# The end of the attention, w_ob and w_out under a hand-written order, with w_out as Strassen's seven products

## The chip, the cores and the metric

The kernel runs on one core of a Trainium2 chip. The metric is device time in microseconds (us) of one execution. The other quantities below come from one execution that the hardware profiler recorded; its span runs from the first to the last instruction, and its own time is a little longer than that span.

The core has TensorE (PE, the matrix engine; its loads of the stationary operand are shown as PEld), VectorE (DVE), ScalarE (ACT), GpSimd (POOL) and SyncE (SP). Here SP only issues transfers. All of them run at once and wait for each other through semaphores. SBUF is the on-chip memory, PSUM holds the matrix engine's results.

## The reference, cut to what matters

One layer has two branches over 1024 latent tokens of width 1024, and 256 context tokens that are only read. Branch A is a gated DeltaNet, branch B a differential softmax attention with 8 heads. Both end in the same way:

```python
y_a = rms_norm(o_a, gdn_norm_w) * silu(z_a)                     # (1024 tokens, 1024)
y_b = rms_norm(o_b, diff_norm_w) * (1 - lambda_init) * silu(z_b)
merged = g_a * (y_a @ w_oa) + g_b * (y_b @ w_ob)                # g_a, g_b: sigmoid gates
out = x + gate * (merged @ w_out)                               # gate: one number per channel
```

w_oa, w_ob and w_out are 1024 x 1024, and everything is float32. This case is about the last two lines and the last head of the attention.

## The kernel before, in words

**Matrix products.** A float32 operand is split in two: hi is a copy rounded to the type that PE reads fast (fp32r), lo is the rest. ACT makes hi, and DVE or POOL makes lo by a subtraction. A product then takes three matmuls for each 128 input channels: hi·hi, hi·lo and lo·hi. All matmuls go through `mm` (L55), all transposes through `tr` (L58); the profile therefore shows them under these two lines, and they are told apart by the names of their tiles.

**Order.** The work of the attention is written as generators ("streams"). Each one yields an instruction with its engine, an estimate of its time and what it waits for. `turn_flow` keeps a clock for each engine and always emits the instruction that can start earliest; the bias of a stream decides between those that could start at the same moment. So the order on each engine is fixed when the kernel is built, and on the chip each engine runs its own list in order. The estimates distinguish `DVE` from `DV2` (a DVE instruction with two SBUF operands, which is not planned beside one of POOL), and `DMA` is issued by SP.

**The attention.** For each of 8 heads and each of 8 blocks of 128 queries, `scores` (tile s) makes both score matrices over 1280 keys, `score_out` (L1557) evacuates them, `soft` (L1570) takes the exponential, `scale` (L1587) and `add` (L1594) combine the two maps, `turns` transposes the result (tile t, L58), `high` and `low` split it (L1626, L1631), and `att_out` multiplies it with the values (tile v). When a head has all its blocks, `norm_` computes the inverse norm (POOL, tile bry, L172), turns it (tile m, L58), sends it through memory to spread it over the partitions (rbd, rr), multiplies the head (POOL, L1714) and stores it in `yb`.

**w_oa.** `merge_` multiplies branch A's heads with w_oa beside the attention, in 16 groups (2 halves of 512 tokens times 8 blocks of 128 output channels) of 24 matmuls with 512 moving columns (tile ma), using one PSUM bank, `pbank`. `merge_out` gates a group and stores it in memory (`ma`). With `KEEP = 3` the last three groups are left over.

**The end, `phase3`.** It starts when the hand-written order is over and has its own pools. Here the tile framework orders the work. It runs the three left groups of w_oa (`branch_a`, L1814); it loads every head from `yb` (L1865) and splits it (L1868 on ACT, L1869 alternately on POOL and DVE); then w_ob follows in 16 groups of 24 matmuls (tile m, 512 columns), each with a gate and an addition on DVE (L1896, L1897) and a split of the merged result (L1898, L1899). w_out then comes in four stretches of 256 output channels (tile mo): for each block of 128 tokens 24 matmuls with 256 moving columns, whose sum DVE multiplies with the gate (L1920) and POOL or DVE adds to x (L1925, L1922), before it is stored. The splits of w_ob and w_out are in `split_small` (L1823, L1824).

Of the kernel before, what the change touches and what calls it, by code (L numbers as in the profile page):

```python
# [17 lines left out]
P = 128  # L18
# [7 lines left out]
H = 8  # L26
# [17 lines left out]
class Block:  # L44
# [665 lines left out]
    def run(self):  # L710
# [4 lines left out]
        with ExitStack() as left:  # L715
# [981 lines left out]
    def norm_(self, h, w, t, to):  # L1697
# [4 lines left out]
        yield lambda: self.pbank  # L1702
        b = self.pbank.pop(0)
        pm = self.pm.tile([P, 512], F32, tag="mm", name="m")
# [3 lines left out]
        self.pbank.append(e)  # L1708
# [3 lines left out]
        for k in range(4):  # L1712
            s = slice(k * W, (k + 1) * W)
            t = yield POOL, 0.69, [e, to], lambda: nc.gpsimd.tensor_tensor(w["oT"][:, s], w["oT"][:, s], rr[:, s], ALU.mult)  # L1714
        self.rrfree = t
        self.kept[h] = yield DMA, 1.46, [t], lambda: nc.sync.dma_start(self.yb[h], w["oT"])
# [33 lines left out]
    def side_weights(self):  # L1750
# [11 lines left out]
        for i, p in enumerate(todo):  # L1762
# [39 lines left out]
    def branch_a(self, o, m):  # L1802

        nc = self.nc
        os = slice(o * 512, o * 512 + 512)
        g = self.yr.tile([P, 512], F32, tag="g", name="g")
        nc.sync.dma_start(g, self.gt[m][:, os])
        _, hi, lo = self.ready_["a", o, m]
        pt = self.pm.tile([P, 512], F32, tag="mm", name="ma")
        for k in range(KT):  # L1810
            _, yh, yl = self.ready_["y", o, k]
            for i, (x, y) in enumerate(((hi, yh), (hi, yl), (lo, yh))):
                self.mm(pt, x[:, k], y, k == i == 0, k == KT - 1 and i == 2)
        nc.vector.tensor_tensor(g, pt, g, ALU.mult)  # L1814
        nc.sync.dma_start(self.ma[m][:, os], g)

    def split_small(self, raw, shape):

        nc, n = self.nc, shape[0] // 2
        hi, lo = (self.ws.tile([P, *shape], F32R, tag=t, name=t) for t in ("wh", "wl"))  # L1820
        for s in range(2):
            k = slice(s * n, s * n + n)
            nc.scalar.copy(hi[:, k], raw[:, k])  # L1823
            (nc.vector, nc.gpsimd)[s].tensor_tensor(lo[:, k], raw[:, k], hi[:, k].bitcast(F32), ALU.subtract)  # L1824
        return hi, lo

    def load_small(self, src):
        raw = self.wr.tile([P, KT, P], F32, tag="wr", name="wr")
        self.nc.sync.dma_start(raw, src.rearrange("(k p) n -> p k n", p=P))
        return self.split_small(raw, (KT, P))  # L1830

    def phase3(self, side):

        nc, a = self.nc, self.a
        with ExitStack() as st:
            mp, yr = self.spool(st, "mp", side="right"), self.spool(st, "yr3", 2, side="right")
            self.wr = self.spool(st, "wr3", 2, side="right")
            self.pm = self.spool(st, "pm3", 6, space=PSUM)
            mh, ml = {}, {}
            left = [(g, a["w_oa"][0, :, g[2] * P:(g[2] + 1) * P]) for g in self.groups]  # L1840
            left += [(("b", m), a["w_ob"][0, :, m * P:(m + 1) * P]) for m in range(KT)]
            for o in range(2):
                for h in range(H):
                    assert ("y", o, h) in self.ready_
            wt = {}

            def fetch(i):
                if i < len(left):
                    g, src = left[i]
                    wt[g] = self.ready_[g][1:] if g in self.ready_ else self.load_small(src)  # L1850

            def out_load(u):
                ws = self.ws
                self.ws = wf if u % 2 == 0 else ws
                raw = wf.tile([P, KT, W], F32, tag="wr", name="wr", bufs=1)
                nc.sync.dma_start(raw, a["w_out"][0, :, u * W:(u + 1) * W].rearrange("(k p) n -> p k n", p=P))
                wt["o", u] = [self.split_small(raw[:, k:k + 4], (4, W)) for k in (0, 4)]
                self.ws = ws
            with ExitStack() as sy:
# [10 lines left out]
                for i, (g, _) in enumerate(left):  # L1870
# [5 lines left out]
                    if g[1] == 0:  # L1876
                        side.close()
                        wf = self.spool(st, "wf", 2)
# [97 lines left out]
```

## Time and profile before

| what | value |
|---|---|
| median of 3 runs | 2034.13 us (2033.2 to 2037.52) |
| the profiled execution: its own time | 2031.96 us |
| its span | 2030.2 us |
| PE busy | 1959.4 us, 97% of the span |
| DVE busy | 1407.7 us, 69% |
| ACT busy | 1058.0 us, 52% |
| POOL busy | 688.7 us, 34% |
| granted clock of PE, mean | 0.991 |

"Busy" counts the time in which at least one instruction of the engine is running. The matmuls of PE overlap: a matmul with 512 columns is recorded with about 390 ns, though in a dense stretch the next one starts after some 230 ns. So the busy share says little about PE's pace; what one matmul costs is read from the distance between starts.

### The profile page before, as it was taken

How to read it: one execution, taken by the hardware profiler on the slowest of the kernel's cores; microseconds unless marked ns; L12 is line 12 of the kernel's file. 1: busy time of each engine (PE TensorE's matmuls, PEld its weight loads, DVE VectorE, ACT ScalarE, POOL GpSimd, SP SyncE). 2: the span in 40 equal slices, each digit the busy share in tenths (PEclk: the TensorE clock that was granted, in tenths of full speed). 3: DMA queues.
4: the chain of work that ended last, by engine and by line, in shares of the span. 5: the costliest groups of instructions: out<-in, count | busy, mean ns of one | idle time of the engine just before them, and what ended most of it. 6: DMA issues, size and time to landing. Idle time of an engine off the chain costs nothing.

```text
span 2030.2 us, 38407 instructions
## 1 busy us (share of the span) xinstructions
PE 1959.4 (97%) x14239; PEld 1722.5 (85%) x14239; DVE 1407.7 (69%) x3581; ACT 1058.0 (52%) x2184; POOL 688.7 (34%) x618
## 2 busy tenths in 40 slices
PE   6999999999999999999989999999899999989999
PEld 4988888899999988788778888887788888877899
DVE  4797989858877876458647874347779999764532
ACT  4453444353334625656466555448678888763210
POOL 3200000024522323232323242335666766654122
PEclk9999999999999999999999999999999999999999
DMA  9253463566356554767575664857475855326442
GB/s 319 61 162 85 130 145 100 132 219 182 105 169 216 183 190 105 235 198 237 138 229 180 222 192 137 250 156 208 120 197 125 240 154 147 105 94 209 134 156 84
DMA packets 393474, 337.49 MB, mean 166 GB/s; under 512 B 144594, under 2 KB 343860, under 8 KB 393288
## 3 DMA queue, kind: packets, MB, share of 16 engines
q1 hardware_dynamic: 329351, 274.22, 46.0%
q10 hardware_dynamic: 63936, 60.83, 9.7%
q8 instruction: 112, 1.84, 0.4%
q14 instruction: 75, 0.61, 0.1%
HBM read 222.66 MB, written 112.32 MB: 165 GB/s over the span
## 4 chain that ended last, share of the span: by engine, by line
PE 72%; DMA 10%; DVE 8%; ACT 5%; issue 2%; SPq 1%; POOL 1%; ACTq 0%; DVEq 0%; POOLq 0%
PE mm L55 37%; PE chain L55 5%; PE mo L55 4%; PE s L55 4%; PE v L55 4%; PE m L55 4%; PE out L55 3%; PE ma L55 3%; DVE S L1557 3%; PE t L58 2%; ACT S L1570 2%; DMA wr<-in_w_in_dram 1%; DVE al L1631 1%; DMA vv<-gv 1%; PE gram L55 1%
## 5 line engine op out<-in xcount | busy, mean ns | idle before, releaser
L55 PE MATMUL mm<-hs,wh 128*128 128x512 f32 (+1 forms) x2048 | 649.4, 391 | 2.1 <-DVE hs L403 1.4
L55 PEld LDWEIGHTS mm<-hs,wh 128*128 128x128 f32 x2048 | 373.1, 190 | 61.3 <-issue 2.2
L55 PE MATMUL mm<-hs,wl 128*128 128x512 f32 (+1 forms) x1024 | 401.2, 392 | 0.0
L55 PE MATMUL mm<-wh,hs 128*128 128x256 f32 (+1 forms) x1792 | 334.8, 286 | 0.0
L55 PEld LDWEIGHTS mm<-wh,hs 128*128 128x128 f32 x1792 | 281.5, 191 | 0.4
L1557 DVE TENSOR_SCALAR_CACHE_REDUCE S<-s,rsq 128x512 f32<-128x512 f32 (+1 forms) x384 | 241.8, 655 | 33.1 <-PE s L55 30.6
L55 PE MATMUL mm<-wl,hs 128*128 128x256 f32 (+1 forms) x896 | 256.0, 286 | 0.0
L1594 POOL TENSOR_TENSOR S<-S 128x1280 f32<-128x1280 f32 x64 | 188.9, 2955 | 90.9 <-ACT S L1587 85.0
L55 PEld LDWEIGHTS mm<-hs,wl 128*128 128x128 f32 x1024 | 195.0, 190 | 28.9 <-issue 0.9
L1570 ACT ACTIVATE S<-S,mn 128x1280 f32<-128x1280 f32 x128 | 174.7, 1366 | 34.3 <-DVE mn L1569 33.6
L55 PEld LDWEIGHTS mm<-wl,hs 128*128 128x128 f32 x896 | 171.2, 191 | 0.3
L590 DVE SCALAR_TENSOR_TENSOR ac<-xc,convT,ac 128x1284 f32<-128x1284 f32 (+1 forms) x96 | 138.7, 1448 | 16.2 <-ACT ac L588 15.6
L55 PE MATMUL s<-kk,qh 128*128 128x512 f32 (+1 forms) x384 | 145.1, 379 | 3.1 <-DVE S L1557 2.8
L55 PE MATMUL s<-kk,ql 128*128 128x512 f32 (+1 forms) x384 | 134.2, 360 | 0.0
L1631 DVE TENSOR_TENSOR al<-t,ah 128x512 fp32r<-128x512 f32 (+1 forms) x192 | 107.6, 593 | 10.0 <-ACT ah L1626 9.4
L575 POOL MEMSET xc<- 128x2 f32 (+1 forms) x64 | 3.6, 101 | 301.8 <-ACT sq L624 103.4
L1626 ACT CAST ah<-t 128x512 fp32r<-128x512 f32 (+1 forms) x192 | 89.9, 515 | 30.0 <-PE t L58 28.4
L1152 DVE TENSOR_TENSOR tmp<-ab,ts 80x31 f32<-80x31 f32 (+15 forms) x248 | 98.3, 397 | 8.8 <-DMA ab<-da 3.3
L578 ACT COPY xc<-mm 128x512 f32<-128x512 f32 (+1 forms) x64 | 33.3, 534 | 127.5 <-PE mm L55 106.8
L58 PE MATMUL t<-ct,S 128*128 128x128 f32 x640 | 96.1, 276 | 3.0 <-POOL S L1594 1.6
L1330 DVE SCALAR_TENSOR_TENSOR S<-S,egl,chain 128x128 f32<-128x128 f32 x128 | 43.1, 345 | 79.5 <-PE chain L55 76.6
L1317 ACT ACTIVATE vd<-chain,edk 128x128 f32<-128x128 f32 x144 | 52.2, 369 | 84.1 <-PE chain L55 81.0
(271 smaller groups left out, 4596.1 us busy)
## 6 DMA issues: line engine op xcount, KB each, us to landing
wr<-in_w_in_dram ACTq DMA_DIRECT2D x44, 512.0 KB
hx<-in_w_in_dram ACTq DMA_DIRECT2D x64, 256.0 KB
X<-gcd SPq DMA_DIRECT2D x16, 640.0 KB
kd<-col SPq DMA_DIRECT2D x40, 256.0 KB
xd<-X SPq DMA_DIRECT2D x16, 640.0 KB
x<-xd SPq DMA_DIRECT2D x80, 128.0 KB
kk<-kd SPq DMA_DIRECT2D x32, 320.0 KB
wa<-in_w_ada_dram SPq DMA_DIRECT2D x8, 1024.0 KB
```

The source lines that it names most:

```text
L55: self.nc.tensor.matmul(out, lhsT, rhs, start=start, stop=stop)
L58: self.nc.tensor.transpose(out, src, self.ident[:src.shape[0], :src.shape[0]])
L578: e = yield ACT, 0.57 if m == 512 else 0.31, [t, x["old"]], lambda: nc.scalar.copy(xc[:, d:d + m], pt[:, :m])
L590: t = yield DV2, 1.21e-3 * wd, [t], lambda: nc.vector.scalar_tensor_tensor(ac[:, :wd], xc[:, j:j + wd], self.convw(j, x["ct"]), ac[:, :wd] ...
L1152: t = yield DV2, n * w / 960.0 + 0.08, [t, t1], lambda: V.tensor_tensor(tv, ab[:, j + 1:, j:j + 1].to_broadcast([80, n, w]), ts[:, j, :w]. ...
L1317: td = yield ACT, 0.251, [t], lambda: nc.scalar.activation(vd, pc[:, 1], AF.Copy, scale=self.edk[:, c, g:g + 1])
L1330: t = yield DVE, 0.263, [t], lambda: V.scalar_tensor_tensor(Sn, S, self.egl[:, c, g:g + 1], pc[:, 2], ALU.mult, ALU.add)
L1557: e = yield DVE, 0.675 if m == 512 else 0.408, [e, self.sfree[c].get(n - 4 + c)], lambda: self.nc.vector.tensor_scalar(x["S"][c][:, o:o + ...
L1570: x["x"].append((yield ACT, 1.36, [e], lambda: nc.scalar.activation(S, S, AF.Exp, bias=x["mn"][:, c:c + 1], scale=-1.0, accum_out=w["l0"][ ...
L1594: e = yield POOL, 2.9, [e], lambda: self.nc.gpsimd.tensor_tensor(S0, S0, S1, ALU.add)
L1626: e = yield ACT, 0.48 if nb == 4 else 0.27, [t, y["old", k]], lambda: self.nc.scalar.copy(y["ah", k][:, :, q], pv)
L1631: t = yield DVE, 0.603 if k < 2 else 0.322, [e, y["old", k]], lambda: self.nc.vector.tensor_tensor(y["al", k][:, :, q], pv, y["ah", k][:, ...
```

## The change

The hand-written order no longer ends with the attention: it runs to the last store of the kernel, and `phase3` goes.

- **Last head.** Head 7 isn't stored in `yb` and loaded again: `y_split` splits it from the tile `oT` in place. The other heads are loaded into the tile of their lo part, and the subtraction overwrites it ("in place").
- **w_oa.** The last three groups stay in `merge_`, which may take them up as soon as all scores have been emitted (`scored == H * NL`). They use the one PSUM bank of `merge_`.
- **w_ob.** `b_main` has the same 384 matmuls as before. The first three groups run head by head, side by side in three banks that the scores have released; the others follow one by one. `b_out` gates and adds, and keeps the merged result `mt` in SBUF in float32.
- **w_out.** With `mt` and w_out cut into quarters (512 channels by 512 tokens, 512 by 512), the product takes seven products of sums of quarters rather than eight (Winograd's form of Strassen's method). Each has 4 blocks of 128 tokens, times 4 blocks of channels, times 3 matmuls with 512 moving columns: 48, and 336 in all instead of 768 with 256 columns. `w_fetch` multiplies w_out with the gate once, so that the results no longer need it. `prep_a` and `prep_b` form the sums (`w_sum`, DVE) and split them (`w_split`, ACT and DVE) into two pairs of slots: operands i reuse the slots of i - 2 and wait for that product's last matmul (`free_`). `o_out` adds the products up with x, on DVE and POOL, and stores 16 tiles of 128 x 512.
- **Pools.** `closing` releases and opens pools in three stages as their users finish. The attention's pools `a0` and `a2` change places.

The core of the diff, with "..." where lines are left out:

```diff
@@ -786,13 +786,14 @@
-            with ExitStack() as st, zr:
-                self.att_more(st)
-                self.wq, self.pm = self.spool(st, "wq", 2), self.spool(st, "pm4", 1, space=PSUM)
-                with tc.manual_schedule(engines={E.PE, E.DVE, E.Activation, E.Pool, E.SP}):
-                    self.side_start()
-                    self.turn_flow(lambda: len(self.kept) == H and not self.mouts)
-        self.phase3(side)
+            st = ExitStack()
+            self.att_more(st)
+            self.wq, self.pm = self.spool(st, "wq", 2), self.spool(st, "pm4", 1, space=PSUM)
+            with tc.manual_schedule(engines={E.PE, E.DVE, E.Activation, E.Pool, E.SP}):
+                self.side_start()
+                self.last_start(zr, st, side)
+                self.turn_flow(lambda: self.last_done == 4 * NL // 2)
+            zr.close()
 
@@ -1408,8 +1409,10 @@
-        self.a0, self.a2 = self.spool(st, "a0", side="right"), self.spool(st, "a2", 2, side="right")
-        self.aps = self.spool(st, "aps", 3, side="right", space=PSUM)
+        self.a2 = self.spool(st, "a2", 2, side="right")
+        self.a0s, self.apss = st.enter_context(ExitStack()), st.enter_context(ExitStack())
+        self.a0 = self.spool(self.a0s, "a0", side="right")
+        self.aps = self.spool(self.apss, "aps", 3, side="right", space=PSUM)
...
-        pm = self.pm.tile([P, 512], F32, tag="mm", name="m")
+        yield lambda: self.pbank or h == H - 1 and self.fb
+        if self.pbank:
+            b, back = self.pbank.pop(0), self.pbank.append
+            pm = self.pm.tile([P, 512], F32, tag="mm", name="m")
+        else:
+            pm, b, back = self.lbank("m")
...
+            e1 = t if k == 1 else e1 if k else None
-        self.kept[h] = yield DMA, 1.46, [t], lambda: nc.sync.dma_start(self.yb[h], w["oT"])
+        if h == H - 1:
+            self.o_last, self.kept[h] = w["oT"], [[e1], [t]]
+        else:
+            self.kept[h] = yield DMA, 1.46, [t], lambda: nc.sync.dma_start(self.yb[h], w["oT"])
...
-            if i + 1 < len(todo) - self.KEEP + 2:
+            if i + 1 < len(todo):
-        while len(self.groups) > self.KEEP:
+        while self.groups:
             _, o, m = g = self.groups[0]
+            yield lambda: len(self.groups) > self.KEEP or self.scored == H * NL
...
+    def last_start(self, zr, st, side):
...
+        for g, b in ((self.closing(zr, st, side), 200), (self.y_split(), 201), (self.b_weights(), 202), (self.forever(self.bouts), 203),
+                     (self.b_gates(), 204), (self.w_first(), 206), (self.w_more(0), 206), (self.w_more(1), 210), *((self.forever(q), 204.5) for q in self.oq),
+                     (self.prep_a(0), 205), (self.prep_b(0), 205), (self.prep_a(1), 210), (self.prep_b(1), 210), (self.x_loads(), 209), (self.b_main(), 220), (self.o_main(), 221)):
+            self.stream(g, b)
...
+    def closing(self, zr, st, side):
+
+        yield lambda: self.scored == H * NL and not self.evs
+        self.apss.close()
+        px = self.spool(zr, "px", 1, side="right", space=PSUM)
+        self.fb += [(px, f"x{i}", None) for i in range(3)]
+        yield lambda: min(self.vdone) == H * NL // 2
+        self.a0s.close()
+        self.bp = self.spool(zr, "bp", side="right")
+        for n in "hl":
+            self.bp.tile([P, 4, 512], F32R, tag=f"b{n}", name="b" + n)
+        sy = zr.enter_context(ExitStack())
+        self.yq, self.stage = self.spool(sy, "yq", side="right"), 1
+        yield lambda: H - 1 in self.yk and not self.groups and not self.mouts and self.wdone >= 16
+        st.close()
+        side.close()
+        pl = self.spool(self.ctx, "pl", 1, space=PSUM)
+        self.fb += [(pl, f"l{i}", None) for i in range(5)]
+        self.lp, self.stage = self.spool(self.ctx, "lp"), 2
+        self.mt = self.lp.tile([P, KT, L], F32, name="mt")
+        yield lambda: self.bdone == 2 * KT
+        sy.close()
+        self.rp, self.stage = self.spool(zr, "rp", side="right"), 3
+
+    def y_split(self):
...
+        for h in range(H):
+            (yh, yl), last = ys[h], h == H - 1
+            yield lambda: h in self.kept
+            if not last:
+                raw = yl.bitcast(F32)
+                ts.append([(yield DMA, 1.46, [self.kept[h]], lambda: nc.sync.dma_start(raw, self.yb[h]))] * 2)
+                if h < 5:
+                    continue
+            for g in range(6) if h == 5 else (h,):
+                (yh, yl), ends = ys[g], []
+                raw = self.o_last if last else yl.bitcast(F32)
+                t = self.kept[g] if last else ts[g]
+                for o in range(2 if last else 1):
+                    c = slice(o * 512, o * 512 + 512) if last else slice(0, L)
+                    t1 = yield ACT, 0.57 if last else 1.06, [t[o]], lambda: nc.scalar.copy(yh[:, c], raw[:, c])
+                    t2 = yield DV2, 0.65 if last else 1.25, [t1], lambda: nc.vector.tensor_tensor(
+                        yl[:, c], raw[:, c], yh[:, c].bitcast(F32), ALU.subtract)
+    def b_main(self):
...
+        first = [(m, o) for m in range(KT) for o in range(2)][:3]
+        seq = [(h, *g) for h in range(3) for g in first[:2]] + [(h, *first[2]) for h in range(3)]
+        seq += [(h, *g) for h in range(3, H) for g in first]
+        seq += [(h, m, o) for m in range(1, KT) for o in range(m == 1, 2) for h in range(H)]
...
+    def b_out(self, m, o, pt, t, back):
...
+        t = yield DVE, 0.605, [t, tg], lambda: V.tensor_tensor(g, pt, g, ALU.mult)
+        back(t)
+        t = yield DV2, 0.65, [t, tm], lambda: V.tensor_tensor(self.mt[:, m, os], g, self.mt[:, m, os], ALU.add)
...
-    def phase3(self, side):
...
+    def w_split(self, n, i, src, deps):
+
+        nc, (hi, lo), ends = self.nc, self.lslot(i, n), []
+        for s in range(2):
+            k = slice(2 * s, 2 * s + 2)
+            t1 = yield ACT, 1.06, deps, lambda: nc.scalar.copy(hi[:, k], src[:, k])
+            t2 = yield DV2, 1.25, [t1], lambda: nc.vector.tensor_tensor(lo[:, k], src[:, k], hi[:, k].bitcast(F32), ALU.subtract)
+            ends += [t1, t2]
+        self.ops_[n, i] = hi, lo, ends
+        return ends
+    def w_sum(self, out, x, y, op, deps):
+
+        ends = []
+        for s in range(2):
+            k = slice(2 * s, 2 * s + 2)
+            ends.append((yield DV2, 1.25, deps, lambda: self.nc.vector.tensor_tensor(out[:, k], x[:, k], y[:, k], op)))
+        return ends
+    def prep_a(self, part):
...
+        s1 = self.rp.tile([P, 4, 512], F32, name="s1")
+        yield from self.w_split("a", 1, q(1, 0), d(1, 0))
+        t1 = self.sums_[1] = yield from self.w_sum(s1, q(0, 1), q(1, 1), ALU.add, d(0, 1) + d(1, 1))
+        f = yield from self.free_(2)
+        t2 = yield from self.w_split("a", 2, s1, [t1, f])
+        t1 = yield from self.w_sum(s1, s1, q(0, 0), ALU.subtract, [t2])
+        f = yield from self.free_(3)
+        t2 = yield from self.w_split("a", 3, s1, [t1, f])
+        t1 = yield from self.w_sum(s1, q(1, 0), s1, ALU.subtract, [t2])
...
+    def prep_b(self, part):
...
+            self.sums_[13] = yield from self.w_sum(w12, w22, w12, ALU.subtract, [self.sums_[11], t22])
...
+        t1 = self.sums_[11] = yield from self.w_sum(w11, w12, w11, ALU.subtract, [t12, self.w11_t])
+        f = yield from self.free_(2)
+        t2 = yield from self.w_split("b", 2, w11, [t1, f])
...
+        t1 = yield from self.w_sum(w11, w22, w11, ALU.subtract, [t2, t22])
+        f = yield from self.free_(3)
+        t2 = yield from self.w_split("b", 3, w11, [t1, f])
+        t1 = yield from self.w_sum(w11, w11, w21, ALU.subtract, [t2, t21])
+        f = yield from self.free_(4)
+        yield from self.w_split("b", 4, w22, [t22, f])
...
+    def o_main(self):
...
+        for i, (bank, tok, name) in enumerate([(Z, bz, "z") if i == 2 else (X, bx, "x") for i in range(7)]):
+            yield lambda: ("a", i) in self.ops_ and ("b", i) in self.ops_
+            (ah, al, ta), (bh, bl, tb) = self.ops_["a", i], self.ops_["b", i]
+            key = {1: 0, 3: 1, 4: 3, 5: 4, 6: 5}.get(i)
...
+                ts = slice(t * P, t * P + P)
+                for k in range(4):
+                    for j, (x, y) in enumerate(((ah, bh), (ah, bl), (al, bh))):
+                        e = yield PE, 0.2265, [ta, tb, d], lambda: self.mm(
+                            bank[t], x[:, k, ts], y[:, k], k == j == 0, k == 3 and j == 2)
...
+    def o_out(self, i, t, X, Z, e):
...
+        if i == 0:
+            p = self.p1[t] = self.rp.tile([P, 512], F32, name=f"p1{t}")
+            e = self.ot[0, t] = yield ACT, 0.57, [e], lambda: nc.scalar.copy(p, X)
+            yield lambda: (0, 0, t) in self.xt
+            x, tx = self.xt[0, 0, t]
+            self.ot[0.5, t] = yield DV2, 0.65, [e, tx], lambda: V.tensor_tensor(x, p, x, ALU.add)
+        elif i == 1:
+            x = self.xt[0, 0, t][0]
+            e = self.ot[1, t] = yield DVE, 0.605, [e, self.ot[0.5, t]], lambda: V.tensor_tensor(x, X, x, ALU.add)
+            self.xfree[0, 0, t] = yield from self.put(0, 0, t, x, e)
+        elif i == 3:
+            u, v = self.rp.tile([P, 512], F32, name=f"u2{t}"), self.p1[t]
+            self.u2[t] = u
...
+            self.ot[3.5, t] = self.xfree[0, 1, t] = yield POOL, 1.3, [e, tx], lambda: nc.gpsimd.tensor_tensor(v, v, x, ALU.add)
...
+        elif i == 5:
+            u = self.u2[t]
...
+            x, tx = self.xt[1, 1, t]
+            e = yield POOL, 1.3, [e, tx], lambda: nc.gpsimd.tensor_tensor(x, u, x, ALU.add)
+            e2 = yield DVE, 0.605, [e], lambda: V.tensor_tensor(x, Z, x, ALU.add)
...
+            x1, tx = self.xt[1, 0, t]
...
+            e = yield DVE, 0.605, [e, self.ot[5.5, t]], lambda: V.tensor_tensor(u, u, X, ALU.subtract)
+            yield from self.put(1, 0, t, u, e)
```

More of the change, by code (lines that the diff above doesn't have):

```diff
@@ new lines, in y_split @@
+    def y_split(self):
+        nc = self.nc
+        yield lambda: self.stage
+        ys = [[self.yq.tile([P, L], F32R, tag=f"{n}{h}", name=n) for n in ("yh", "yl")] for h in range(H)]
+        ts = []
+        for h in range(H):
[16 more added lines that the diff above has]
+                    ends += [t1, t2]
+                self.yk[g] = yh, yl, ends
@@ new lines, in b_weights @@
+    def b_weights(self):
+        nc = self.nc
+        yield lambda: self.stage
+        xr, free = self.gh[0].tile([P, 2, KT, P], F32, tag="X", name="wr"), [None, None]
+        fetch = lambda m: (DMA, 1.46, [free[m % 2]], lambda: nc.sync.dma_start(
+            xr[:, m % 2], self.a["w_ob"][0, :, m * P:(m + 1) * P].rearrange("(k p) n -> p k n", p=P)))
+        ts = [(yield fetch(0)), (yield fetch(1))]
+        for m in range(KT):
+            yield lambda: self.wdone >= 15 + m
+            hi, lo = (self.ws.tile([P, KT, P], F32R, tag=n, name=n) for n in ("wh", "wl"))
+            ends = []
+            for s in range(2):
+                k = slice(4 * s, 4 * s + 4)
+                t1 = yield ACT, 0.52, [ts[m], self.wfree.get(14 + m)], lambda: nc.scalar.copy(hi[:, k], xr[:, m % 2, k])
+                t2 = yield DV2, 0.62, [t1], lambda: nc.vector.tensor_tensor(
+                    lo[:, k], xr[:, m % 2, k], hi[:, k].bitcast(F32), ALU.subtract)
+                ends += [t1, t2]
+            self.bh[m], free[m % 2] = (hi, lo, ends), ends
+            if m + 2 < KT:
+                ts.append((yield fetch(m + 2)))
+        self.xr_t = ends
@@ new lines, in b_gates @@
+    def b_gates(self):
+        nc = self.nc
+        yield lambda: self.stage >= 2
+        for i in range(2 * KT):
+            m, o = divmod(i, 2)
+            os = slice(o * 512, o * 512 + 512)
+            yield lambda: len(self.gfree_b) > i - 2 and (i < 3 or H - 1 in self.yk)
+            g = self.lp.tile([P, 512], F32, tag=f"g{i % 2}", name="g")
+            tg = yield DMA, 0.73, [self.gfree_b[i - 2] if i > 1 else None], lambda: nc.sync.dma_start(g, self.gt[KT + m][:, os])
+            tm = yield DMA, 0.73, [], lambda: nc.sync.dma_start(self.mt[:, m, os], self.ma[m][:, os])
+            self.gates_b[m, o] = g, tg, tm
@@ new lines, in w_sum, with w_first @@
+    def w_sum(self, out, x, y, op, deps):
+        ends = []
+        for s in range(2):
+            k = slice(2 * s, 2 * s + 2)
+            ends.append((yield DV2, 1.25, deps, lambda: self.nc.vector.tensor_tensor(out[:, k], x[:, k], y[:, k], op)))
+        return ends
+    def w_first(self):
+        nc = self.nc
+        yield lambda: self.stage
+        self.gb = self.gh[0].tile([P, D], F32, tag="qk", name="gb")
+        self.gb_t = yield DMA, 1.46, [], lambda: nc.sync.dma_start(self.gb, self.gad[:, :].to_broadcast([P, D]))
+        self.w21 = self.gh[0].tile([P, 4, 512], F32, tag="kq", name="w21")
+        yield lambda: self.stage >= 2 and self.bdone > 6
+        self.w11 = self.lp.tile([P, 4, 512], F32, name="w11")
+        t = yield from self.w_fetch(self.w11, 0, 0, [])
+        self.w11_t = yield from self.w_split("b", 0, self.w11, [t])
+        t = yield from self.w_fetch(self.w21, 1, 0, [])
+        self.w21_t = yield from self.w_split("b", 1, self.w21, [t])
@@ new lines, in x_loads @@
+    def x_loads(self):
+        nc = self.nc
+        yield lambda: self.stage == 3
+        order = [(0, n, t) for n in range(2) for t in range(4)] + [(1, n, t) for t in range(4) for n in (1, 0)]
+        for i, (th, n, t) in enumerate(order):
+            yield lambda: i < 8 or order[i - 8] in self.xfree
+            x = self.rp.tile([P, 512], F32, tag=f"x{i % 8}", name="x")
+            self.xt[th, n, t] = x, (yield DMA, 0.73, [self.xfree.get(order[i - 8]) if i > 7 else None], lambda: nc.sync.dma_start(
+                x, self.a["x"][0, (4 * th + t) * P:(4 * th + t + 1) * P, n * 512:n * 512 + 512]))
```

238 lines of the change are left out of this document (122 added, 116 removed).

## The prediction

> **What bounds the kernel now.** After the page I read busy time and granted clock in six stretches of the end.
>
> ```profile
> span 2030.2 us, 38407 instructions
> ...
> 1802.80:1822.20 19.40, 13.68 (x97) 12.38 (x96) 8.52 (x23) 8.81 (x18) 6.47 (x3) 0.91 0.49 157
> 1822.20:1840.20 18.00, 18.00 (x73) 14.73 (x74) 5.22 (x6) 4.19 (x6) 8.08 (x7) 0.91 0.45 152
> 1840.20:1871.40 31.20, 26.79 (x105) 20.17 (x103) 13.67 (x13) 12.32 (x17) 13.90 (x8) 0.95 0.64 221
> 1871.40:1937.00 65.60, 65.59 (x282) 52.87 (x283) 34.77 (x46) 13.24 (x23) 7.55 (x6) 1.00 0.46 144
> 1937.00:2026.60 89.60, 89.60 (x769) 89.40 (x767) 22.64 (x44) 6.85 (x12) 23.95 (x12) 1.00 0.38 121
> 2026.60:2030.20 3.60, 0.00 (x1) 0.00 (x0) 0.85 (x2) 0.00 (x0) 0.00 (x0) 1.00 0.11 36
> ```
>
> After the length, the columns are busy time of PE, PEld, DVE, ACT and POOL, then granted clock, DMA share and GB/s. From 1871 on PE never stops, and DVE is busy for 57.4 of those 155.2 us: PE sets the end there. In the first three rows PE stands still in parts, and its clock drops. The waits of PE (total, times, longest) and the chain of waits (start, length) say why.
>
> ```profile
> PE m L55 <- POOL yl L1869: 2.4, 2, 1.2
> PE m L58 <- POOL bry L172: 2.0, 1, 2.0
> PE m L55 <- ACT yh L1868: 1.6, 1, 1.6
> ...
> 1808.87 2.90 POOL S L1594
> ...
> 1813.87 4.66 PE v L55 x29
> ...
> 1820.46 1.65 POOL bry L172
> ...
> 1822.16 0.27 PE m L58
> 1822.43 7.10 PE ma L55 x24
> ...
> 1840.90 3.60 DMA y<-yb
> ...
> 1848.04 5.44 DMA y<-yb
> ...
> 1857.05 10.69 PE m L55 x38
> ...
> 2026.64 0.43 DVE ro L1920
> ...
> 2027.10 0.42 DVE ro L1922
> ```
>
> The last head's norm holds PE until 1822; then w_ob waits for heads that are loaded and split two at a time. Behind each stop matmuls are slow: 24 of w_oa took 7.10 us, 38 of w_ob 10.69.
>
> **What a matmul costs.** Instructions of one tile in dense stretches, with their count (ma, m, mo), and ten transposes from the chain:
>
> ```profile
> 1826.50:1839.50 13.00, 13.00 (x59) 1.00 0.46 156
> ...
> 1872.00:1935.00 63.00, 63.00 (x272) 1.00 0.45 141
> ...
> 1940.00:2020.00 80.00, 80.00 (x688) 1.00 0.38 121
> ...
> 1756.23 1.09 PE t L58 x10
> ```
>
> A record lasts 0.39 us with 512 columns and 0.28 with 256, so some 1.7 or 2.4 of each count belong to the edges: ma 13.0/57.3 = 0.2267 us, m 63.0/270.3 = 0.2331, mo 80.0/685.6 = 0.1167. The two rows with 512 columns differ by 3% at the same clock, and nothing in the trace says why. Per column mo costs what m costs (2 x 0.1167 = 0.2334). So wider columns are worth between nothing and 3%; what surely falls is the number of products, by an eighth. I take 0.230 for w_ob and w_out, halfway, since either row could be theirs, with 0.2267 and 0.2331 as ends.
>
> **The change part by part**, counted from 1802.8, the end of the scores' matmuls.
>
> *End of attention and w_oa.* PE still owes the attention 60 matmuls of 256 columns (7.0 us by mo's 0.1167), 26 transposes (2.8 by the ten above) and the norm's small ones (1.2 and 0.27):
>
> ```profile
> L55 PE MATMUL v<-ah,vh 128*128 128x256 f32 x20 | 6.5, 323 | 0.0
> ...
> L58 PE MATMUL t<-ct,S 128*128 128x128 f32 x26 | 3.9, 292 | 2.0 <-POOL S L1594 1.6 <-DVE mn L1569 0.5
> L55 PE MATMUL v<-ct,osq 128*128 128x1 f32 x8 | 1.2, 255 | 1.5 <-DVE oT L1668 1.5
> ```
>
> 11.3 us in all. The three groups of w_oa, 72 x 0.2267 = 16.3 us, now fill the holes. But they share one bank, so each waits until DVE has gated the one before:
>
> ```profile
> 1829.55 0.70 DVE g L1814
> ```
>
> That is about 1 us with the signals on both sides; two such turns fall behind the attention's last matmul. With a few tenths elsewhere I put PE's idle time at 3.5 us. Bounds are 1 (other work fills the turns) and the 19.4 - 11.3 = 8.1 us of before, which also cover the case that the split of the sixteenth block of w_oa, two instructions of 1.30 on POOL, stands ahead of the last S addition (2.90). w_ob starts at 1802.8 + 11.3 + 16.3 + 3.5 = 1833.9.
>
> *Heads.* Their tiles lie where the attention's were, so loads begin behind the last v matmul, at 1818.5. Six heads and two blocks of w_ob go out together, 4 MB:
>
> ```profile
> 1845.00:1850.00 5.00, 3.85 (x17) 1.00 1.02 337
> ...
> 1824.00 0.33 SPq L1711 DMA_DIRECT2D rr<-rbd  x1
> ...
> L1868 ACT CAST yh<-y 128x1024 fp32r<-128x1024 f32 x8 | 8.3, 1049 | 10.8 <-DMA y<-yb 10.8
> ...
> L1714 POOL TENSOR_TENSOR oT<-oT,rr 128x256 f32<-128x256 f32 x32 | 22.6, 741 | 10.5 <-DMA rr<-rbd 10.5
> ```
>
> At 337 GB/s they have landed by about 1833, the first by about 1822 (3.60 after its issue). SP issues in order, and head 7's rr, at about 1824, queues behind them: 1835, then four multiplications on POOL (3.0) and its split in place, about 1840. Head 6 is loaded only after head 5's split is emitted: 1834 + 3.6 + 2.3 = 1840. PE takes 9 x 0.230 = 2.1 us per head over the first three groups and asks for head 6 at 1833.9 + 12.4 = 1846.3. So w_oa's last groups and six heads hide all of it, with 6 us to spare; beyond these each late us costs one. The stalls on yl and yh, and the store and load of head 7, are gone.
>
> *w_ob.* 384 x 0.230 = 88.3 us (87.1 to 89.5): it ends at 1922.2 instead of 1937.0. Beside it DVE gates and adds (two instructions per group of 5.5 us), splits the blocks of w_ob and the first quarters of w_out, and POOL scales three quarters of w_out: half of DVE's time at most, so nothing on the path.
>
> *w_out.* 336 x 0.230 = 77.3 us (76.2 to 78.3) for 89.6. Whether PE gets them without stops is DVE's matter, since operands i can be split only when product i - 2 is over. The prices:
>
> ```profile
> 60.11 1.21 DVE L312 TENSOR_TENSOR wl<-wr,wh 128x1024 fp32r<-128x1024 f32 x1
> 61.24 0.28 DVE L312 TENSOR_TENSOR wl<-grw,wh 128x128 fp32r<-128x128 f32 x1
> ...
> 1834.99 0.69 DVE L1814 TENSOR_TENSOR g<-ma,g 128x512 f32<-128x512 f32 x1 [4.15 <-PE ma L55]
> 1835.60 0.68 DVE L1824 TENSOR_TENSOR wl<-wr,wh 128x512 fp32r<-128x512 f32 x1
> ...
> L1769 POOL TENSOR_TENSOR wl<-wq,wh 128x512 fp32r<-128x512 f32 x30 | 38.6, 1296 | 27.8 <-ACT wh L1768 26.3 <-DVE rl L1578 1.3
> ...
> L1869 DVE TENSOR_TENSOR yl<-y,yh 128x1024 fp32r<-128x1024 f32 x4 | 9.1, 2283 | 14.9 <-ACT yh L1868 14.9
> ```
>
> From start to start an instruction on 1024 elements takes 1.13 us and one on 512 takes 0.61. Between the end of w_ob and the start of the sixth product DVE has 34 of the first kind (18 for the splits of a1 to a5 and b2 to b5, 14 for sums, 2 for scaling the last quarter of w_out) and 18 of the second (2 for the last group of w_ob, 16 for results): 38.4 + 11.0 = 49.4 us. POOL's four additions in that time, 1.30 each, may hold it back by 5.2. That makes 54.6, against five products of 48 x 0.230 = 55.2 us: DVE is as full as PE. Each of five releases also begins with ACT's copy (1.05, some 1.25 with signals), in which DVE may have nothing to do: 6.3 us at worst. The last product needs only two more splits, 4.5 us in 11. I take 3 us of stops. They can't be negative; the upper end is 10: the 6.3, and 52 x 0.08 = 4.2 if the records' lengths count and not their distances, less the 0.6 to spare.
>
> [...]
>
> *Tail.* Before, 3.6 us from the last matmul to the end with two DVE instructions of 0.43; after, one of 0.69 and a last store of 256 KB instead of 128: 3.7 (3.4 to 4.2). The other transfers move about as many bytes as before (121 to 144 GB/s of the 337 seen) beside the matmuls.
>
> *Sum.* 1922.2 + 77.3 + 3.0 + 3.7 = 2006.2 against 2030.2: **24.0 us less**, 14.8 of it up to the end of w_ob and 9.2 behind. The profiled execution's own time is 2031.96, 2.2 below the median of the runs, 2034.13. Less 24.0 this is 2008 by the one and **2010** by the other; I predict 2010, since medians are compared.
>
> **The rivals.**
>
> *DVE paces w_out.* If its waits come in full, stops are 10 us and the time is 2017. For it: the count above leaves no slack. Against it: sums can run ahead of a release, and two pairs of slots give each pair of splits a whole product.
>
> *The heads come late.* If the chain to head 6 or 7 grows by 15 us, the 6 us of cover go and 9 are lost: 2019. For it: a pair of loads took up to 5.44 us before, and head 6's load is emitted late. Against it: the six loads queue in one go.
>
> *DVE locked out, slower.* Beside POOL's subtractions the same instruction took 2.28 us on DVE (yl). At this price throughout w_out, 34 x 2.28 + 11.0 = 88.5 us against 55.2: stops of 33 rather than 3, and 2040, 6 us slower than before. It decides from 27 us of stops, that is from a mean of (55.2 + 27 - 11.0)/34 = 2.1 us. Against it: POOL has 12 additions, 15.6 us, in all of w_out and can't stand beside every one.
>
> *Narrower gaps everywhere.* 0.2267 in w_ob and w_out (2.4 us less), 1 us of idle time (2.5), no stops (3.0): 2002. Against it: m's row, and the count of DVE. [...]
>
> **How the numbers follow.** Forecast 0.62 (own range 2003 to 2015), DVE paces 0.16, late heads 0.10, locked out 0.06, narrower gaps 0.06. The range from 2001 to 2022 leaves out the slower case and the tails of the two before it. A change under 0.2%, 4 us, is less than a measurement of this kernel can tell from none. Faster 0.89: all cases but the locked one and the far tails of the two others; same 0.04; slower 0.07.
>
> **What would show it.** Right: w_oa's matmuls among the attention's after 1803, with PE's clock at 1.00 up to 1840; w_ob over by about 1922; matmuls 0.227 to 0.233 apart in w_out, with short waits for lo parts only. Wrong: PE waiting for yl behind 1840 (heads); long waits of PE at the third to sixth product (DVE's count); DVE subtractions of 2 us there (lock-out); or a shift ahead of 1800, where I expect none though two pools change places.

## The result, and the profile after

| | before | after |
|---|---|---|
| median, 4 runs each on one chip | 2033.8 us (2033.2 to 2037.52) | 2005.67 us (2000.92 to 2007.8) |
| span of the profiled execution | 2030.2 us | 2002.3 us |

The changed kernel takes 0.9855 of the time before (95% interval 0.9832 to 0.9877): 28.1 us less, where 24.0 had been forecast. A second measurement beside another run of the kernel before gave 0.9848 (0.9828 to 0.9868).

From the page of the kernel after, its span; then the chain of waits (start, length, what):

```profile
span 2002.3 us, 37575 instructions
```
```profile
1826.63 5.75 PE ma L55 x24
1832.38 89.60 PE mb L55 x384
1921.99 21.84 PE x L55 x96
1943.82 10.91 PE z L55 x48
1954.74 43.66 PE x L55 x192
1998.49 0.69 DVE u L2156
```

mb is w_ob, x and z are w_out. From 1832.38 to 1998.49 the chain holds nothing but matmuls. All that PE waited for from 1780 to 2003 (total, times, longest):

```profile
PE ma L55 <- DVE g L1808: 0.8, 1, 0.8
PE s L55 <- DVE S L1560: 0.4, 1, 0.4
PE v L55 <- DVE oT L1671: 0.2, 1, 0.2
```

The stages, with busy time of PE, PEld, DVE, ACT, POOL, then clock, DMA share and GB/s. The first row runs from the scores' end to w_ob, the second is w_ob, then come the first six of the seven products and the tail:

```profile
1803.64:1832.20 28.56, 27.78 (x169) 24.20 (x168) 18.07 (x34) 17.64 (x28) 9.13 (x5) 1.00 0.63 211
...
1832.20:1922.00 89.80, 89.80 (x386) 72.15 (x385) 48.29 (x59) 18.77 (x27) 18.04 (x10) 1.00 0.58 194
...
1922.00:1932.90 10.90, 10.90 (x49) 8.98 (x49) 8.77 (x10) 1.76 (x3) 0.00 (x0) 1.00 0.60 206
1932.90:1943.80 10.90, 10.90 (x50) 8.99 (x49) 10.90 (x13) 4.52 (x6) 0.00 (x0) 1.00 0.19 72
1943.80:1954.70 10.90, 10.90 (x50) 9.00 (x49) 10.90 (x11) 4.09 (x5) 0.00 (x0) 1.00 0.34 122
1954.70:1965.60 10.90, 10.90 (x50) 9.00 (x49) 10.83 (x13) 3.87 (x5) 3.99 (x3) 1.00 0.07 24
1965.60:1976.60 11.00, 11.00 (x50) 9.09 (x49) 10.79 (x12) 4.19 (x5) 3.92 (x2) 1.00 0.40 144
1976.60:1987.50 10.90, 10.90 (x49) 9.00 (x48) 8.72 (x11) 3.73 (x4) 5.82 (x4) 1.00 0.19 74
...
1998.40:2002.30 3.90, 0.00 (x0) 0.00 (x0) 0.69 (x1) 0.00 (x0) 0.00 (x0) 0.84 0.17 67
```

PE stands still for 0.78 us in the first row and not at all below it, at full clock. DVE works through 43.4 of the 43.7 us of the second to fifth product, and yet PE never waits for it. By stage, from the end of the scores' matmuls (1802.80 before, 1803.64 after):

| stage | before | forecast | after |
|---|---|---|---|
| up to w_ob | 37.4 | 31.1 | 28.6 |
| w_ob | 96.8 | 88.3 | 89.8 |
| w_out, stops with it | 89.6 | 80.3 | 76.4 |
| tail | 3.6 | 3.7 | 3.9 |
| sum | 227.4 | 203.4 | 198.7 |

### The profile page after: what moved, and what is told of

The parts are those of the page before. It is cut to its first block, busy times and chain, and to the rows that moved or that the text cites. A ratio compares the mean times of both kernels' runs of the same rounds, so it can differ in the third digit from the quotient of the medians.

```text
span 2002.3 us, 37575 instructions
## 1 busy us (share of the span) xinstructions
PE 1940.0 (97%) x13807; PEld 1692.7 (85%) x13807; DVE 1457.0 (73%) x3613; ACT 1071.5 (54%) x2187; POOL 673.9 (34%) x610
## 4 chain that ended last, share of the span: by engine, by line
PE 73%; DVE 10%; DMA 8%; ACT 4%; issue 2%; SPq 1%; POOL 1%; ACTq 0%; DVEq 0%; POOLq 0%
PE mm L55 37%; PE chain L55 5%; PE v L55 5%; PE mb L55 4%; PE s L55 4%; PE ma L55 3%; PE x L55 3%; DVE S L1560 3%; PE out L55 3%; PE t L58 2%; DMA hx<-in_w_in_dram 1%; PE gram L55 1%; DVE al L1634 1%; ACT S L1573 1%; DVE ac L590 1%
## 5 line engine op out<-in xcount | busy, mean ns | idle before, releaser
L1597 POOL TENSOR_TENSOR S<-S 128x1280 f32<-128x1280 f32 x64 | 188.8, 2952 | 90.2 <-ACT S L1590 87.7
```

Source lines behind the costliest of these rows:

```text
L1597: e = yield POOL, 2.9, [e], lambda: self.nc.gpsimd.tensor_tensor(S0, S0, S1, ALU.add)
```

## The experiments

All are edits of the changed kernel. Single executions differ ahead of the place of these edits: one piece of w_oa's work, seven matmuls ma in the chain of waits, began between 1745.95 and 1753.56 in the runs. So I count two stretches that repeat to 0.1 us: from that piece to the first matmul of w_ob, and from there to the end of the span. Where an edit moves a stretch by more, I read it as the edit's doing, although behind each edited kernel but the one with the pad stands a single execution.

| kernel | piece begins | up to w_ob | w_ob to end |
|---|---|---|---|
| changed | 1750.67 | 81.5 | 170.1 |
| changed, measured again (e9) | 1753.56 | 81.5 | 170.1 |
| eight products (e1) | 1750.39 | 81.5 | 181.0 |
| 256 columns (e2) | 1749.07 | 81.5 | 175.6 |
| groups held (e3) | 1748.31 | 96.4 | 170.1 |
| groups and loads held (e3b) | 1745.95 | 87.7 | 170.2 |
| heads moved by 32 bytes (e4) | 1749.61 | 81.5 | 167.5 |
| the same, timed (e8) | 1750.51 | 81.6 | 167.5 |
| weights moved by 32 bytes (e10) | 1748.88 | 81.6 | 169.6 |
| more work on DVE (e5) | 1747.36 | 81.5 | 176.2 |
| last head through memory (e6b) | 1746.56 | 81.5 | 177.1 |
| parts' weights moved too (e7) | 1752.78 | 81.5 | 167.5 |

### What w_out's gain consists of

Eight products in place of seven: `prep_a` and `prep_b` only split quarters, and pairs of products share a bank.

```diff
-        for i, (bank, tok, name) in enumerate([(Z, bz, "z") if i == 2 else (X, bx, "x") for i in range(7)]):
+        for i in range(8):
+            g, kh = i // 2, i % 2
+            bank, tok, name = (Z, bz, "z") if g % 2 else (X, bx, "x")
...
-                            bank[t], x[:, k, ts], y[:, k], k == j == 0, k == 3 and j == 2)
+                            bank[t], x[:, k, ts], y[:, k], kh == k == j == 0, kh == 1 and k == 3 and j == 2)
```

> w_out as eight plain products of halves with the same 512 moving columns in the same order of banks, with no sums of operands; every quarter of x and of w_out is split once and used twice. It computes the same output. The prediction's theory: the gain behind w_ob is the number of matmuls alone, so 48 more of the 0.2274 us that they took in the changed kernel come back: PE's stretch of w_out grows from 76.4 to 87.3 us, the span by 10.9 us to 2013.2. Rival 1: the eighth product was never the point, the gain came from 512 columns in place of 256: then the stretch stays within 2 us of 76.4. Rival 2: DVE, full over three products in the changed kernel, holds PE by stops that the intervals hide; without the sums PE's matmuls then come closer and the stretch grows by clearly less than 10.9 us.

Seven products with narrow matmuls:

```diff
-                for k in range(4):
+                for c in (slice(0, 256), slice(256, 512)):
+                    for k in range(4):
...
-                            bank[t], x[:, k, ts], y[:, k], k == j == 0, k == 3 and j == 2)
+                                bank[t][:, c], x[:, k, ts], y[:, k, c], k == j == 0, k == 3 and j == 2)
```

> Strassen's seven products stay, but each matmul of w_out is cut into two of 256 moving columns (672 in place of 336), with the same operands and output. Theory: 512 columns are worth little by themselves; by the 0.1167 us of w_out's matmuls in the kernel before the stretch becomes 78.4 us (+2.0), by the 0.120 us that other matmuls of 256 columns took in the same traces 80.6 us (+4.2). Rival: the wider matmul is the larger part of the gain, and the stretch grows by 9 us or more. Second rival: DVE paces w_out, and the stretch stays at 76.4 us.

The chain of the kernel with eight products:

```profile
1921.68 21.84 PE x L55 x96
1943.51 21.83 PE z L55 x96
1965.34 21.83 PE x L55 x96
1987.17 21.83 PE z L55 x96
```

And of the kernel with 256 columns, with its one wait in w_out:

```profile
1920.38 23.03 PE x L55 x192
1943.40 11.50 PE z L55 x96
```
```profile
PE x L55 <- DVE bl L1988: 1.1, 1, 1.1
```

Eight products cost 10.9 us more, exactly 48 matmuls of 0.2274: the theory holds and both rivals fall. The narrow matmul takes 23.03/192 = 0.120 us, the upper of the two prices: 4.2 us for 672 of them, and with the wait and what stands around it 5.5. So neither rival holds here: the stretch grew, but far less than 9 us. The one wait is for a half of bl that stands in DVE's order behind a sum of the product before; that sum itself waited 2.2 us for PE. Against the kernel before (89.6 us) eight products with 512 columns (87.3) gain 2.3 us, and seven products in place of eight another 10.9. So the number of products makes 10.9 of the 13.2 us.

### Has DVE any room left?

The prediction counted DVE as full. Here it gets five additions more, into a tile that is no longer read:

```diff
+        if n + str(i) in ("b3", "a4", "b4", "a5", "b5"):
+            yield DV2, 1.25, deps, lambda: nc.vector.tensor_tensor(
+                self.gb.rearrange("p (a b) -> p a b", a=2), src[:, 0:2], src[:, 0:2], ALU.add)
```

> One more addition of 1024 elements on DVE into a tile that nobody reads ahead of each of five splits of w_out (the second operands of products 3, 4 and 5, the first of products 4 and 5, two halves each counted once: two pieces ahead of one split are not added, one is): 5 pieces of 1.14 us from start to start, 5.7 us in all. Theory: DVE is full from product 1 to product 4 and the last split ends less than 1 us before PE wants it, so PE stops and w_out grows by 4.5 to 5.7 us. Rival: DVE's order has slack that busy time does not show (sums that ran ahead), and w_out grows by under 1.5 us.

(One piece stands ahead of each of the five splits.) Its waits, and the last stops in the timeline:

```profile
PE x L55 <- DVE bl L1991: 5.0, 4, 2.7
```
```profile
1978.38 0.50 PE L55 MATMUL x<-bl,ah 128*128 128x512 f32 x1 [2.75 <-DVE bl L1991]
1978.72 0.40 PE L55 MATMUL x<-bh,al 128*128 128x512 f32 x1
...
1980.65 0.50 PE L55 MATMUL x<-bl,ah 128*128 128x512 f32 x1 [0.63 <-DVE bl L1991]
```

5.7 us of work bring 5.0 us of stops, and the stretch grows by 6.1, a little over the 4.5 to 5.7 expected. The rest is how a stop is counted: the idle time runs from the end of a record, which is 0.39 us long where the next matmul would have come after 0.23, and the matmul after the stop is followed at 0.34 us. That adds 0.27 us to each of the four stops, 1.1 in all. So DVE has less than 1 us to spare: it was as full as counted, and the rival of hidden room falls. Why the changed kernel has no stops all the same shows in its own timeline of DVE, at the splits for products 2 and 4, counted from 0, whose first matmuls start at 1943.66 and 1965.49:

```profile
1943.35 1.22 DVE L1988 TENSOR_TENSOR bl<-w,bh 128x1024 fp32r<-128x1024 f32 x1
...
1964.99 1.22 DVE L1988 TENSOR_TENSOR bl<-w,bh 128x1024 fp32r<-128x1024 f32 x1
```

The last half of bl ends 0.9 and 0.7 us after its product has begun; PE has the first half, and needs the second only at the eighth matmul, 1.6 us after the first. That margin, and sums that DVE makes while ACT copies, are what the allowance of 3 us left out.

### What w_oa's last groups are worth

The groups wait, as before the change, for the attention's last value matmul. By the order of the instructions this moves 24 of their 72 matmuls behind it.

```diff
-            yield lambda: len(self.groups) > self.KEEP or self.scored == H * NL
+            yield lambda: len(self.groups) > self.KEEP or self.stage
```

> The last three groups of w_oa are held back until the last value matmul of the attention is out, as in the kernel before; all else is the changed kernel. Theory: the holes that DVE leaves to PE in the last heads' sums open again and the groups follow behind them: w_ob starts 4 to 7 us later than at 1832.4, and the span grows by as much (2006 to 2009). Rival: the groups only moved and the holes were covered by other work anyway: under 1 us.

w_ob starts 14.9 us later by the stretches. PE's waits, and the chain in the middle of them:

```profile
PE v L55 <- DVE oT L1671: 5.0, 3, 4.4
PE ma L55 <- DVE g L1808: 3.2, 2, 2.3
PE t L58 <- POOL S L1597: 1.6, 1, 1.6
```
```profile
1815.66 5.20 DMA yl<-yb
1820.92 1.04 ACT yh L1874
1821.97 0.28 ACT osq L1664
```

Not the 4 to 7 us expected: this is more than the holes. The planner had also put the copies of w_ob's heads ahead of the attention's last output (osq) in ACT's queue; they waited there for loads that came late, and PE waited with them. In DVE's queue the gate of w_oa (g, L1808) stood behind the subtraction of such a head in the same way, which made the wait of 2.3 us. So the second kernel holds the loads back too:

```diff
         nc = self.nc
-        yield lambda: self.stage
+        yield lambda: self.stage and not self.groups
```

> As the run before that held w_oa's last groups (w_ob started 12.5 us later than in the changed kernel), but the loads of the heads for w_ob are also held until the last group of w_oa is out, so that no split of a head stands ahead of the last head's products on DVE. Theory now: of the 12.5 us about 5 to 8 belong to the attention's open holes and the lower clock behind them, the rest (4.4 us before v, 2.3 us before ma) to splits that waited for their loads in DVE's queue: w_ob starts 5 to 8 us later than at 1832.4. Rival: the groups themselves are worth it all, 11 us or more stay. The time of w_ob's start may also show a wait for the first head's load, which now comes later; it is counted apart.

```profile
PE ma L55 <- DVE g L1808: 1.7, 2, 0.9
PE t L58 <- POOL S L1597: 1.6, 1, 1.6
PE v L55 <- DVE oT L1671: 0.6, 2, 0.5
...
```

(The 12.5 us named there compare start times; the stretches say 14.9.) The convoy is gone, and w_ob starts 6.2 us late: within 5 to 8, and the rival falls. 3.4 us of it are waits: 4.8 in all, against the 1.4 of the changed kernel. Of the remaining 2.8, some 1.7, an estimate, are the lower clock (10 x 0.10 + 12 x 0.06), seen in two rows of its windows where the changed kernel has 1.00; at 0.27 us for each of four more stops, as above, 1.1 come on top:

```profile
1800.00:1810.00 10.00, 7.95 (x59) 7.44 (x57) 5.51 (x16) 6.70 (x14) 3.80 (x2) 0.90 0.61 188
1810.00:1822.00 12.00, 11.22 (x63) 9.49 (x62) 3.04 (x7) 2.42 (x6) 2.47 (x2) 0.94 0.07 23
```

### The last head in place

```diff
-        if h == H - 1:
+        if False:
             self.o_last, self.kept[h] = w["oT"], [[e1], [t]]
...
-            (yh, yl), last = ys[h], h == H - 1
+            (yh, yl), last = ys[h], False
```

> The last head too goes through memory: its output is stored, loaded and split like the seven others. Theory: in place it was ready at 1842.9 and PE asked at 1846.9; store and load add some 5 us, so it is ready near 1848: w_ob stops once for 0 to 3 us, and the span grows by no more. Rival 1: the cover is larger than read, nothing changes (within 0.7 us). Rival 2: the split of the late head stands ahead of other work in DVE's and ACT's queues, the weights of w_ob come late behind it, and the span grows by more than 4 us.

In this run (span 2450.4 us) the clock was 0.726 over the whole execution; w_ob took 108.96 us and had no wait, which says nothing on the question. The kernel ran again:

> The same kernel as the one with the last head through memory, since in that run TensorE's granted clock was 0.726 over the whole span, and a slower TensorE asks later for the head. Same theories: one stop of 0 to 3 us in w_ob; rival 1: under 0.7 us; rival 2: more than 4 us, from work that queues behind the late split.

The timeline of PE at its only two waits in w_ob:

```profile
1846.01 0.49 PE L55 MATMUL mb<-yh,wh 128*128 128x512 f32 x1 [3.03 <-ACT yh L1874]
1847.27 0.80 PE L55 MATMUL mb<-yl,wh 128*128 128x512 f32 x1 [0.76 <-DVE yl L1875]
1847.87 0.63 PE L55 MATMUL mb<-yh,wl 128*128 128x512 f32 x1
1848.29 0.63 PE L55 MATMUL mb<-yh,wh 128*128 128x512 f32 x1
1848.72 0.63 PE L55 MATMUL mb<-yl,wh 128*128 128x512 f32 x1
```

PE stands idle for 3.8 us and the stretch grows by 7.0: over all that was expected but rival 2, whose cause it isn't, since no other wait appears. From start to start the two stops cost 4.2 us. Behind them come 14 distances of 0.426 us (5.54/13 from 1847.87 to 1853.41) rather than 0.233, the first a little longer, which cost another 2.9 us; the clock is lower there (0.58 from 1846 to 1850):

```profile
1850.00:1854.00 4.00, 4.00 (x12) 3.13 (x11) 3.90 (x7) 1.04 (x3) 0.00 (x0) 0.57 0.62 196
1854.00:1858.00 4.00, 4.00 (x19) 3.22 (x18) 1.28 (x2) 0.69 (x2) 0.00 (x0) 1.00 0.91 274
```

So the split in place saves 7 us here, and the idle time counts almost double.

### Where w_ob's matmuls lose 3%

By the addresses of the built kernel the heads, w_ob's moving operand, lie 32 bytes off a multiple of 64, the weights on one; in w_oa both lie on one. The kernel before has both matrices placed alike, which fits its 0.2331 and 0.2267. A pad moves the heads:

```diff
         ys = [[self.yq.tile([P, L], F32R, tag=f"{n}{h}", name=n) for n in ("yh", "yl")] for h in range(H)]
+        self.yq.tile([P, 8], F32, tag="pad", name="pad")
```

> A pad of 32 bytes moves the heads' tiles, the moving operand of w_ob, down by 32 bytes, so that their addresses and those of the weights both lie at multiples of 64 bytes; nothing else differs. In the changed kernel w_ob's matmuls follow at 0.2333 us with the moving operand 32 bytes off such a multiple, those of w_oa at 0.2267 us with both on it. Theory of the place in memory: w_ob's matmuls come at 0.2267 us, its 384 take 87.1 us in place of 89.6, the span falls by 2.5 us to 1999.8. Rival: the interval comes from the load of the other engines or from what runs beside it: 0.2333 us and 89.6 us stay.

From its chain, and one group of instructions (min, median and max length, first and last start), first of this kernel and then of the changed one:

```profile
1831.27 87.04 PE mb L55 x384
```
```profile
L55 PE MATMUL mb<-yh,wh x128: 389/389/389, 1831.1 to 1917.5; 128*128 128x512 f32 x128
```
```profile
L55 PE MATMUL mb<-yh,wh x128: 393/396/399, 1832.2 to 1921.1; 128*128 128x512 f32 x128
```

87.04/384 = 0.2267 us: the theory holds. Is it the difference between the two operands that counts? Here the heads stay and the weights move, so that both are off:

```diff
-            hi, lo = (self.ws.tile([P, KT, P], F32R, tag=n, name=n) for n in ("wh", "wl"))
+            hi, lo = (self.ws.tile([P, KT * P + 16], F32R, tag=n, name=n)[:, 8:8 + KT * P].rearrange(
+                "p (k n) -> p k n", n=P) for n in ("wh", "wl"))
```

> The heads' tiles stay where the changed kernel has them, 32 bytes off a multiple of 64, and it is the weights of w_ob, the stationary operand, that move by 32 bytes: now both are off. Theory that only the difference between the two operands counts: the 384 matmuls come at 0.2267 to 0.2274 us (87.1 to 87.3 us in place of 89.6), as with the heads' pad. Rival, that the moving operand must lie on a multiple of 64: 0.2333 us and 89.6 us stay.

```profile
1830.71 88.94 PE mb L55 x384
```

88.94/384 = 0.2316 us lies between: both statements miss. So in w_ob the place of the operands sets the distance (0.2267, 0.2316 or 0.2333 us), and multiples of 64 for both are the best seen. It isn't the whole rule. In w_out the products with odd numbers have both operands 32 bytes off too, those with even numbers have both on a multiple, and the two kinds can't be told apart: product 2, the only one of tile z, takes 10.91/48 = 0.2273 us, all seven on average 0.2274. What else counts stays open.

With 256 columns I looked for the like in the projections beside the recurrence (this kernel has the heads' pad as well):

```diff
-                yield from self.weight(raw, *(self.wab[i % 2].tile([P, KT, W], F32R, tag=n, name=n) for n in ("wh", "wl")),
+                yield from self.weight(raw, *(self.wab[i % 2].tile([P, KT * W + 8], F32R, tag=n, name=n)[:, 8:].rearrange(
+                                           "p (k w) -> p k w", k=KT) for n in ("wh", "wl")),
```

> The kernel with the 32-byte pad, and moreover the weights of the projections that run beside the recurrence shifted by 32 bytes: 1968 matmuls of 256 moving columns have the moving operand 32 bytes off a multiple of 64 and the stationary one on it. With both on it they follow at 0.120 us; the attention's value matmuls, moving on it and stationary 32 bytes off, at 0.1167. Theory 1: at 256 columns any difference of 32 bytes between the two is the faster case: 0.1167 us, and where PE is the bound the span falls by up to 6.5 us. Theory 2: an off moving operand always costs, as it did with 512 columns: 0.1233 us, up to 6.5 us longer. Rival: no change.

The group of these matmuls, first with the heads' pad alone, then with the weights moved:

```profile
L55 PE MATMUL mm<-wh,hs 128*128 128x256 f32 x1632 | 302.5, 285 | 0.0
```
```profile
L55 PE MATMUL mm<-wh,hs 128*128 128x256 f32 x1632 | 300.3, 283 | 0.0
```

A record is shorter by 2 ns. The span was 2001.8 us, 3.2 over the kernel with the pad alone, and so was the beginning of the piece of w_oa: well inside the spread of 7.6 us that all runs show there, so the span decides nothing. The lengths of the records tell more. With hi weights the group is busy for 300.3 us and not for 302.5, with lo weights for 231.0 and not for 232.4, and from 640 us on the median record lasts 281 and 282 ns where it lasted 283. That is 1 to 2 ns of the 3.3 that the first theory says, and against the sign of the second; by how much the matmuls follow each other more closely, these views don't show. Nor did the edit do quite what was expected of it. By the addresses, 288 of the 1968 matmuls, those of the lo weights in one of the two buffers, still had the moving operand on a multiple of 64; and in other projections it moved lo weights that are the stationary operand. There, with 512 columns, the group with hi weights is busy for 610.1 us in place of 603.9 and its mean record lasts 411 ns in place of 407; with lo weights it is 365.3 us in place of 365.5, and 408 ns both times. So in this run the same 32 bytes made records with 256 columns a little shorter and some of those with 512 longer.

The pad, timed beside the changed kernel on one chip:

> The changed kernel with the 32-byte pad, timed. Theory of the place in memory: from w_ob's start to the end 2.6 us less than in the changed kernel (0.9987 of its time), on the same chip. Rival: the difference is lost in what runs differ by ahead of w_oa (up to 3 us between single profiled runs) and the medians do not tell the two apart.

> The changed kernel unchanged, timed on the same chip beside the one with the pad: about 2005.7 us, 0.9855 of the kernel before, as in its first measurement.

With the pad 2001.37 us (1999.44 to 2006.88), 0.9833 of before (0.9812 to 0.9854); without it 2006.26 (2004.42 to 2007.48), 0.9848 (0.9828 to 0.9868). The stretch is 2.6 us shorter in both profiles with it, but the intervals overlap, so the total doesn't prove the version faster.

## Why the prediction was right

**Direction and size.** 24.0 us were forecast and 28.1 came; the time lies inside the likeliest case's own range. All four steps pointed the right way, and the groups of w_oa did run among the attention's matmuls at clock 1.00: 24 of the 72 ahead of its last value matmul, 24 around the last head's norm, and 24 behind. The sum missed by 4.7 us over the four stages, less the 0.8 by which the scores ended later, a shift within the spread of all runs there. The tail was 3.9 for 3.7.

**Idle time ahead of w_ob, 3.5 us.** The stage took 28.6 us rather than 31.1, 2.5 less. Of the two turns at w_oa's bank one shows, 0.8 us; the other lay beside value matmuls. The prediction's lower bound of 1 was the better value.

**Heads with 6 us to spare.** Right in kind. The splits of head 6 and of head 7, from DVE's timeline:

```profile
1836.39 1.23 DVE L1875 TENSOR_TENSOR yl<-yl,yh 128x1024 fp32r<-128x1024 f32 x1 [1.61 <-ACT yh L1874]
1840.81 2.09 DVE L1875 TENSOR_TENSOR yl<-oT,yh 128x512 fp32r<-128x512 f32 x2 [3.19 <-ACT yh L1874]
```

PE takes 9 x 0.2333 = 2.1 us per head from 1832.2 on and so asks for head 6 at 1844.8 and for head 7 at 1846.9. That leaves 7 and 4 us of cover. But "beyond these each late us costs one" was wrong: 3.8 us of idle time cost 7.0, since the clock fell behind the stop, to 0.58 and 0.57 in two rows of 4 us.

**0.230 us a matmul.** Both stages were halfway guesses, and each was at another end: w_ob 89.60/384 = 0.2333 (1.3 us over the forecast), w_out 76.41/336 = 0.2274 (0.9 under). That the two misses nearly cancel is luck. "Nothing in the trace says why" was true of the trace; for w_ob the addresses say it, and the pad shows it (0.2267 with both operands on multiples of 64).

**Stops of 3 us in w_out.** The term that was most wrong: there were none. The count behind it, DVE as full as PE, was right, as the five additions show; the allowance for ACT's copies was not needed. Inside the count two errors partly offset each other. POOL was to hold DVE back by 5.2 us; up to the sixth product only two subtractions were longer, 1.37 and 1.72 us in place of 1.22. And three more additions of results, 1.8 us, fell into that time than were counted. The two rivals that rest on DVE fell: no stops, and no split slowed to 2 us beside POOL, which worked for up to 5.82 us of a product. The group with the longest of all splits in w_out, from the instructions of L1988 between 1954 and 1990:

```profile
L1988 DVE TENSOR_TENSOR al<-mt,ah x4: 1215/1223/1722, 1967.4 to 1979.8; 128x1024 fp32r<-128x1024 f32 x4
```

A record of this group lasts 1.223 us at the median, but the next instruction begins before that is over: the split that starts at 1977.51 is followed at 1978.65, after 1.14 us. So the 4.2 us that the upper end adds for the records' lengths did not come.

**Narrower gaps everywhere.** This rival was nearest in time, but not as told: idle time and stops went, while w_ob kept its wide gaps. With the pad it holds, but for w_out's 0.2274.

## What to carry to other kernels

Where one engine is the bound and another is as full, count both from start to start, and ask which half of an operand is needed first: here a half that was ready 0.9 us after its product had begun cost nothing. Price a stop of the matrix engine from start to start, and add the slow matmuls that may follow it: here 3.8 us of idle time cost 7.0. When a step is moved in an order written by a planner, look at what now stands ahead in the in-order queues of the helpers: the same move cost 6.2 or 14.9 us.

## What the runs showed of the hardware

**A short stop can cost twice.** Behind the stops of 3.03 and 0.76 us in w_ob, matmuls came at 0.426 us until 1853.4, 7.4 us after the first stop's end; the granted clock was 0.58 from 1846 to 1850, 0.57 from 1850 to 1854 and 1.00 behind that. Behind a stop of 2.75 us in w_out (more work on DVE) the next but one came at 0.23, and the clock from 1974 to 1986 was 1.00. In the kernel with groups and loads held it was 0.90 from 1800 to 1810 and 0.94 from 1810 to 1822, where PE had waited for 1.6 us at most in one piece. By these traces the longest single wait doesn't decide; what does, they don't show.

**The distance of matmuls can depend on where operands lie.** In w_ob, with the same work beside them: 0.2267 us with both on multiples of 64 bytes, 0.2333 with the moving one 32 bytes off, 0.2316 with both off. In w_out both on and both off gave the same 0.227. With 256 columns and most of the moving operands 32 bytes off, a mean record of 283 ns rather than 285.
